# Twenty more pairs of projections by seven half-size products, and weight sums by accumulating transfers

## The chip, the cores and the metric

The kernel runs on one core of one Trainium2 chip. The metric is the device time of one execution in microseconds (us). The kernel before takes 956.11 us, the median of three runs (955.99 to 956.37). The engines are called by the names of the profile: PE multiplies matrices, DVE and ACT work element by element, POOL is GpSimd, SP is the queue that issues most transfers.

## The reference

One decoder block on 512 tokens of 1024 features, with 16 learned meta tokens ahead (528 columns), all in 32-bit floats:

```
xn   = rmsnorm(h, norm1_g)
proj = xn @ w_in      # mq mk mv mi mf mo | gq gk gv ga gr | gate_m gate_g
hm   = mlstm(silu(conv(mq)), silu(conv(mk)), mv, mi, mf);  y_m = headnorm(hm) * sigmoid(mo)
hg   = gla(gq, gk, gv, logsigmoid(ga @ g_a2 + b) / 16);    y_g = headnorm(hg) * silu(gr)
h    = h + (sigmoid(gate_m) * (y_m @ w_branch_m) + sigmoid(gate_g) * (y_g @ w_branch_g)) @ w_out
hn   = rmsnorm(h, norm2_g)
h    = h + (silu(hn @ w_ff_gate) * (hn @ w_ff_up)) @ w_ff_down
out  = rmsnorm(h, final_g)[meta tokens dropped]
```

There are 4 heads in each mixer (key width 128, value width 256), and the channel mixer is 2816 wide.

## The kernel before, in words

**Units.** Every weight matrix is cut into units: one DRAM tile `wst[u]` of 128 x 1024 floats (512 KB) that holds the eight 128 x 128 blocks of one block of 128 output features. Activations lie features on partitions, tokens in columns. Each 32-bit product is made of three matmuls: weights and activations are split into a rounded high part and a rest (`whi`, `wlo`; ACT casts the high part, DVE subtracts), and `mm3` adds high x high, high x rest and rest x high. A unit is 8 such triples of 512 columns (`unit_real`), or 16 of 264 where the meta tokens are needed (`unit_all`).

**Order.** All order is written out by hand: the program emits each engine's instructions in one sequence, and every engine (and each queue) works through its own in that order. SP loads raw weight tiles (`load_raw`, L156) into four rotating buffers, five units ahead; a load waits on SP until the tile four units earlier has been split. `ahead` (L183) puts a split three units ahead of its use. Side work (convolution, gates, heads) is written as generators, and `tick()` after each group of matmuls advances them by a step.

**Stages.** The projections and heads of the first mixer (mLSTM), then those of the second (gated linear attention, GLA) mixed with the merge gates `gm`, `gg` and the branch products `bm`, `bg`, then the output projection, then the channel mixer: 5 blocks of gate and up by plain units, 17 blocks by `pair` (L1077), and the down projection.

**A pair by seven products.** `pair` makes two units that share their input (A is the gate's, B the up's) with seven products of half the depth and half the columns instead of eight: Strassen's scheme in Winograd's form. A product is 4 triples of 256 columns (`seven`, L1048), so a pair is 84 matmuls. The products are called q1, q5, q6, p2, p3, p4, p7. Three PSUM banks hold the sums: bz takes p7 and later p4 on top, bx takes q1, q6, q5 and p3, by takes p2. Because later products are added to the same bank, the state of the bank between them is copied out by ACT (s7: bz after p7; s1: bx after q1; s2: after q6; s5: after q5), and PE may add the next product only when the copy has read the bank. DVE joins the parts (c11, c21, c22), ACT applies Silu, and DVE multiplies gate and up (f). The last product of a pair, p3, is made inside the next pair. The weights of the products are sums of halves of A and B, made by `mix_weights` (L1005) on DVE: two tiles of 128 x 1024 (`st.s`, `st.r`), each half by one addition of 512 columns (L1014, L1015, L1018, L1021), then split like the raw tile of A; of B, only one half (`dh`, `dl`) is split.

Of the kernel before, what the change touches and what calls it, by code (L numbers as in the profile page):

```python
# [15 lines left out]
P = 128  # L16
D = 1024
# [26 lines left out]
TW = 532  # L44
NTT = 60
NSTD = 5
LOGEXP = "natural_log_exp_and_others"
# [3 lines left out]
def unit_order():  # L51

    o = [("gates", 0)]
    m = lambda h: [("mq", h), ("mk", h), ("mv", 2 * h), ("mv", 2 * h + 1), ("mo", 2 * h), ("mo", 2 * h + 1)]
    g = lambda h: [("gq", h), ("gk", h), ("gv", 2 * h), ("gv", 2 * h + 1), ("gr", 2 * h), ("gr", 2 * h + 1)]
    for h in range(H):
        o += m(h)
    for h in range(H):
        o += g(h)
        if h in (1, 2):  # L60
            for i in range(4 * h - 4, 4 * h):
                o += [("gm", i)] if i % 2 == 0 else [("gm", i), ("bm", i - 1), ("bm", i)]
    o += [("gg", i) for i in range(8)] + [("bg", i) for i in range(8)]
    return o


ORDER = unit_order()
NUNITS = len(ORDER) + 8 + 44 + 22
FF0 = len(ORDER) + 8
SW0, SW1 = FF0 + 2 * NSTD, FF0 + 44  # L70

# [13 lines left out]
def hybrid_block(ctx: ExitStack, tc: tile.TileContext, xT, wst, par, con, out):  # L85
# [68 lines left out]
    unit_ix, n_raw = [0], [0]  # L154

    def load_raw(u):  # L156
        while n_raw[0] <= u and n_raw[0] < NUNITS:
            r = raws[n_raw[0]] = wpool.tile([P, D], F32, tag="raw", name=nm("raw"), bufs=4)
            nc.sync.dma_start(r, wst[n_raw[0]])
            n_raw[0] += 1  # L160

    def whi(src):
        t = wpool.tile([P, D], F32R, tag="whi", name=nm("whi"), bufs=5)
        S.copy(t, src)  # L164
        return t

    def wlo(src, hi):
        t = wpool.tile([P, D], F32R, tag="wlo", name=nm("wlo"), bufs=5)
        V.tensor_tensor(t, src, hi.bitcast(F32), ALU.subtract)  # L169
        return t  # L170

    def split_hi(u):
        if u < NUNITS:
            splits[u] = [whi(raws[u])]

    def split_lo(u):
        if u < NUNITS:
            splits[u].append(wlo(raws.pop(u), splits[u][0]))


    plan = {}

    def ahead(u, k):  # L183
        if k == 0:
            load_raw(u + 5)
        if (u, k) in plan:
            for f in plan.pop((u, k)):
                f()
        if not SW0 <= u + 3 < SW1:
            if k == 2:  # L190
                split_hi(u + 3)
            elif k == 4:
                split_lo(u + 3)
# [8 lines left out]
    def unit(outs, ah, al):  # L202

        u = unit_ix[0]
        unit_ix[0] += 1
        w = splits.pop(u)
        for k in range(KT):
            for o, c0, c1 in outs:
                mm3(o, w, k, ah[k], al[k], c0, c1, k == 0, k == KT - 1)
            ahead(u, k)  # L210
            tick()

    def unit_all():
        ps = [bank()[:, :HALF], bank()[:, :HALF]]
        scale = X.scale
        unit([(ps[a], a * HALF, (a + 1) * HALF) for a in range(2)], X.h, X.l)
        return ps, scale

    def unit_real(ah=None, al=None):
        o = bank()  # L220
        if ah is None:
            scale = X.scale
            unit([(o, NM, NT)], X.h, X.l)
            return o, scale
        unit([(o, 0, NS)], ah, al)
        return o

# [24 lines left out]
    cn = apool.tile([P, NCON], F32, name="cn")  # L252
    nc.sync.dma_start(cn, con)
    madd = cn[:, K_MADD:K_MADD + NS]
    m01 = cn[:, K_M01:K_M01 + NS]
# [7 lines left out]
    split_lo(0)  # L263

# [54 lines left out]

    def evac(o, ps):  # L320
# [41 lines left out]
    def gate_rows(ps):  # L362
        sel = gts.sel = apool.tile([P, 8, P], F32R, name="sel")
        G.tensor_copy(sel, cn[:, K_SEL:K_SEL + 8].unsqueeze(2).to_broadcast([P, 8, P]))
# [77 lines left out]
    def conv(box, ps, m, isk):  # L442
# [8 lines left out]
        V.tensor_scalar(a, raw[:, 3 + c0:3 + c0 + n], pr[:, col + 3:col + 4], pr[:, C_CB + m:C_CB + m + 1],  # L451
                        op0=ALU.mult, op1=ALU.add)
# [70 lines left out]
    def head_out(num, d2, gcol, gates, hd, dst):  # L523
# [35 lines left out]
        V.tensor_tensor(t, y0, y0, ALU.mult)  # L559
        V.tensor_tensor(t, t, x, ALU.mult)  # L560
        yield 1
        V.tensor_scalar(t, t, -0.5 / 256.0, 1.5, op0=ALU.mult, op1=ALU.add)
        V.tensor_tensor(y0, y0, t, ALU.mult)
        yield 1
        for vt in range(2):
            y = ts[vt]
            V.tensor_tensor(y, y, y0, ALU.mult)
            yield 1
            hi, lo = tt(F32R, NS), tt(F32R, NS)
            S.copy(hi, y)  # L570
            yield 2
            V.tensor_tensor(lo, y, hi.bitcast(F32), ALU.subtract)
            f = 2 * hd + vt
            dst[0][f], dst[1][f] = hi, lo
# [9 lines left out]
    def mlstm(h, q, k, v, gates, dst):  # L584
        while not gts.ready or q.v is None or k.v is None:
            yield 1
        (qh, ql), (kh, kl) = q.v, k.v
        yield 6
        pb, pm = bank(), bank()
        T.matmul(pb, gts.sel[:, h, :], gts.R, start=True, stop=True)  # L590
        T.matmul(pm, gts.sel[:, H + h, :], gts.R, start=True, stop=True)
# [3 lines left out]
        V.tensor_tensor(dia, pb, madd, ALU.add)  # L595
# [3 lines left out]
        wh = apool.tile([P, WTOT], F32R, tag="wh", name=nm("wh"))  # L599
        wl = apool.tile([P, WTOT], F32R, tag="wl", name=nm("wl"))  # L600
# [46 lines left out]
        for vt in range(2):  # L647
# [8 lines left out]
            if vt == 0:  # L656
# [5 lines left out]
                V.tensor_tensor(em, em, em, ALU.mult)  # L662
# [3 lines left out]
    atts = []  # L666

    def gla_decay(h, gq, gk, dk):
# [12 lines left out]
        b = pr[:, C_A2B + h:C_A2B + h + 1]  # L681
        l, z = tt(), tt()
        for a in range(2):
            c = slice(a * HALF, (a + 1) * HALF)
            act(l[:, c], ps[a], AF.Abs, bias=b)
            V.tensor_scalar(z[:, c], ps[a], b, 0.0, op0=ALU.add, op1=ALU.min)
# [5 lines left out]
        V.tensor_tensor(z, z, l, ALU.subtract)  # L692
# [9 lines left out]
        act(ex[:, 0, :4], bc[:, CH - 1:c4:CH], AF.Exp, scale=1.0 / TAU)  # L702
        act(ex[:, 1, :4], bc[:, mid:c4:CH], AF.Exp, scale=1.0 / TAU)
        act(ex[:, 1, 4:5], bc[:, c4 + 7:c4 + 8], AF.Exp, scale=1.0 / TAU)
# [655 lines left out]
```

## Time and profile before

| | before |
|---|---|
| median of the runs | 956.11 us |
| the profiled execution's own time | 956.21 us |
| its span | 954.2 us |
| PE busy, share of the span | 935.1 us, 98% |
| DVE busy | 601.2 us, 63% |
| ACT busy | 467.6 us, 49% |
| POOL busy | 11.7 us, 1% |
| transferred | 89.40 MB, mean 94 GB/s |

The span runs from the first to the last instruction; the profiled execution's time is 2.0 us longer. Busy time of PE is nearly all of the span, but a matmul's record overlaps the next one's, so the pace of matmuls is read from how many start in a stretch of time. The list of waits names the instruction that an engine stood still for; for SP it is the queue's own waits before it issues a transfer.

### The profile page before, as it was taken

Reading aid. Unit: us, or ns where it says so; the run is one execution under the profiler, and the core shown is the slowest. Engines: PE = TensorE matmul, PEld = TensorE weight load, DVE = VectorE, ACT = ScalarE, POOL = GpSimd, SP = SyncE. Lnnn points to the kernel's source line nnn. Section 1 sums busy time; section 2 is a strip of 40 time slices with the busy share of each in tenths; the row PEclk is TensorE's granted clock in tenths of the full one; section 3 lists DMA queues with packets and bytes.
Section 4 is the critical chain, followed back from the end, with each engine's and each line's share of the span. In section 5 each row is a group of like instructions: output and inputs, shape, how many; then the busy total and the mean of one; then the engine's idle time right before and its main releaser. Section 6 shows DMA issues by size and latency. Waiting matters only on the chain.

```text
span 954.2 us, 13802 instructions
## 1 busy us (share of the span) xinstructions
PE 935.1 (98%) x5687; PEld 832.8 (87%) x5687; DVE 601.2 (63%) x876; ACT 467.6 (49%) x778; POOL 11.7 (1%) x30
## 2 busy tenths in 40 slices
PE   6999999999999999999999999999999999999995
PEld 6988989898988898889888888879999999888885
DVE  6898877674854543452354555798888887842323
ACT  7457667675552544262442234445555555732321
POOL 0000000000000000000000000010000000000000
PEclk9999999999999999999999999999999999999998
DMA  7322221212223232233223343223334233422202
GB/s 262 110 89 69 87 89 45 89 50 84 71 70 94 81 88 85 66 111 89 67 67 110 111 136 129 67 89 105 117 90 129 93 111 112 133 90 87 89 1 88
DMA packets 27294, 89.40 MB, mean 94 GB/s; under 512 B 3040, under 2 KB 5088, under 8 KB 27232
## 3 DMA queue, kind: packets, MB, share of 16 engines
q1 hardware_dynamic: 26144, 87.49, 29.2%
q10 hardware_dynamic: 1088, 1.05, 0.3%
q8 instruction: 44, 0.72, 0.3%
q14 instruction: 18, 0.15, 0.1%
HBM read 86.43 MB, written 2.10 MB: 93 GB/s over the span
## 4 chain that ended last, share of the span: by engine, by line
PE 88%; DVE 8%; ACT 2%; issue 1%; DMA 1%; SPq 0%; DVEq 0%
PE b L198 21%; PE b L200 21%; PE b L199 21%; PE b L1055 6%; PE b L1056 6%; PE b L1054 6%; DVE wlo L169 1%; PE b L767 1%; ACT t L116 1%; PE b L769 1%; PE b L746 1%; PE b L653 1%; PE b L486 1%; PE b L654 1%; DMA t<-xT 1%
## 5 line engine op out<-in xcount | busy, mean ns | idle before, releaser
L198 PE MATMUL b<-t,whi 128*128 128x512 f32 (+2 forms) x1222 | 434.9, 356 | 6.9 <-ACT t L116 6.9
L200 PE MATMUL b<-t,wlo 128*128 128x512 f32 (+2 forms) x1222 | 427.4, 350 | 0.7 <-DVE wlo L169 0.7
L199 PE MATMUL b<-t,whi 128*128 128x512 f32 (+2 forms) x1222 | 427.0, 349 | 0.7 <-DVE t L272 0.7
L198 PEld LDWEIGHTS b<-t,whi 128*128 128x128 f32 x1222 | 231.2, 189 | 36.2 <-ACT t L116 6.8
L200 PEld LDWEIGHTS b<-t,wlo 128*128 128x128 f32 x1222 | 230.8, 189 | 32.6 <-DVE wlo L169 1.1
L199 PEld LDWEIGHTS b<-t,whi 128*128 128x128 f32 x1222 | 231.3, 189 | 30.4 <-DVE t L272 1.0
L169 DVE TENSOR_TENSOR wlo<-raw,whi 128x1024 fp32r<-128x1024 f32 x138 | 168.2, 1223 | 96.0 <-ACT whi L164 95.9
L164 ACT CAST whi<-raw 128x1024 fp32r<-128x1024 f32 x138 | 142.9, 1047 | 17.7 <-issue 7.1
L1056 PE MATMUL b<-t,wlo 128*128 128x256 f32 x408 | 114.6, 281 | 0.0
L1055 PE MATMUL b<-t,whi 128*128 128x256 f32 x408 | 114.5, 281 | 0.0
L1054 PE MATMUL b<-t,whi 128*128 128x256 f32 x408 | 114.2, 280 | 0.0
L1054 PEld LDWEIGHTS b<-t,whi 128*128 128x128 f32 x408 | 76.9, 188 | 0.1
L1055 PEld LDWEIGHTS b<-t,whi 128*128 128x128 f32 x408 | 76.8, 188 | 0.1
L1056 PEld LDWEIGHTS b<-t,wlo 128*128 128x128 f32 x408 | 76.7, 188 | 0.0
L116 ACT ACTIVATE t<-t 128x512 f32<-128x512 f32 (+3 forms) x78 | 43.7, 579 | 45.0 <-DVE t L553 19.5
L116 ACT ACTIVATE t<-b 128x512 f32<-128x512 f32 (+1 forms) x65 | 33.5, 541 | 55.6 <-PE b L200 23.2
L169 DVE TENSOR_TENSOR wlo<-ws,whi 128x1024 fp32r<-128x1024 f32 x34 | 41.5, 1221 | 7.4 <-ACT whi L164 7.4
L116 ACT ACTIVATE t<-f 128x256 f32<-128x256 f32 (+1 forms) x24 | 11.6, 482 | 67.2 <-DVE f L1205 67.2
L1070 ACT COPY t<-b 128x256 f32<-128x256 f32 x51 | 19.0, 373 | 45.6 <-PE b L1056 45.6
L1205 DVE TENSOR_TENSOR f<-f,b 128x512 f32<-128x512 f32 (+1 forms) x9 | 5.7, 629 | 53.9 <-PE b L200 53.9
L164 ACT CAST whi<-ws 128x1024 fp32r<-128x1024 f32 x34 | 35.8, 1052 | 6.3 <-DVE ws L1021 3.5
L791 DVE TENSOR_TENSOR t<-b,t 128x512 f32<-128x512 f32 x16 | 11.1, 691 | 30.8 <-PE b L200 30.8
(200 smaller groups left out, 958.0 us busy)
## 6 DMA issues: line engine op xcount, KB each, us to landing
raw<-wst SPq DMA_DIRECT2D x155, 512.0 KB, 3.5
t<-xT SPq DMA_DIRECT2D x8, 264.0 KB, 5.6
t<-xT SPq DMA_DIRECT2D x8, 256.0 KB, 3.7
out<-t SPq DMA_DIRECT2D x4, 256.0 KB, 2.3
out<-t ACTq DMA_DIRECT2D x4, 256.0 KB, 2.5
cn<-con SPq DMA_DIRECT2D x1, 516.0 KB, 7.3
pr<-par SPq DMA_DIRECT2D x1, 320.0 KB, 7.1
pr<-par SPq DMA_DIRECT2D x1, 44.0 KB, 1.9
```

The costliest lines, as they stand in the source:

```text
L116: S.activation(o, i, func, **kw)
L164: S.copy(t, src)
L169: V.tensor_tensor(t, src, hi.bitcast(F32), ALU.subtract)
L198: T.matmul(o, w_h, ah[:, c0:c1], start=first, stop=False)
L199: T.matmul(o, w_h, al[:, c0:c1], start=False, stop=False)
L200: T.matmul(o, w_l, ah[:, c0:c1], start=False, stop=last)
L486: T.transpose(pb[:, c * P:(c + 1) * P], f[:, c * CH:(c + 1) * CH], ident)
L791: V.tensor_tensor(t, ps, t, ALU.mult)
L1054: T.matmul(o, h, xh_[k], start=start and k == 0, stop=False, skip_group_check=not start)
L1055: T.matmul(o, h, xl_[k], start=False, stop=False, skip_group_check=not start)
L1056: T.matmul(o, l, xh_[k], start=False, stop=k == 3, skip_group_check=not start)
L1070: s7=lambda: S.copy(s[:, lo], bz), s1=lambda: S.copy(s[:, hi], bx), s2=lambda: S.copy(r[:, lo], bx),
```

## The change

The seven-product scheme of the channel mixer is written once for all and used for 20 more pairs: of each GLA head q with k, the two v units and the two r units (12 pairs), and the merge gates `gm` and `gg` two by two (8 pairs). Pairs of q, k and v work on halves of 272 columns (`ALL`), the others on halves of 256 (`REAL`). The order of units in the second mixer changes: all gates `gm` and head 0 come first, then all of `bm`, then heads 1 to 3 interleaved, `gg` and `bg`.

Two of the four half sums of a pair (`ws` first half: B's first half plus A's; `wr` first half: B's two halves) are no longer made by DVE: SP loads one addend from DRAM into the sum's buffer, and POOL issues a transfer that adds the other (`sum_tile`, L198 of the new kernel). `ws` and `wr` have one buffer each, raw tiles three in place of four, `whi` and `wlo` four in place of five. The order of the seven products is now p7, q1, p3 of the pair before, q6, p4, p2, q5 (before: p7, p3 of the pair before, q1, p4, q6, p2, q5).

`begin` loads raw tiles up to `u + 5` and hangs the weight work of the next pair at places of the present one, called by product and step (`("p4", 2)` is p4 after its third triple). Work on `ws` is called b (`b_sum`, `b_hi`, `b_lo`), on the raw tile of A a (`a_hi`, `a_lo`), on half of B d, on `wr` c (`c_hi`, `c_lo`). The work on c is done inside the pair that uses it. New activation sums for the second mixer are made once (`mixed_x`) during the last mLSTM heads. Several small DVE operations go to ACT (first tap of the convolution, clamp of the GLA decay by Relu, squares, state scaling), branch inputs are split later (`parts`), and the two masks share one buffer.

```diff
-    o += [("gg", i) for i in range(8)] + [("bg", i) for i in range(8)]
+    two = lambda n, i: [((n, 2 * i), (n, 2 * i + 1))]
+    g = lambda h: [(("gq", h), ("gk", h))] + two("gv", h) + two("gr", h)
+    bm = lambda i: one(("bm", 2 * i), ("bm", 2 * i + 1))
+    o += two("gm", 0) + two("gm", 1) + g(0) + two("gm", 2) + two("gm", 3)
+    for i in range(4):
+        o += bm(i)
+    q, v, r = ([g(h)[i] for h in range(H)] for i in range(3))
+    o += [q[1], v[1], q[2], r[1], v[2], q[3], r[2], v[3]] + two("gg", 0) + [r[3]]
...
     def load_raw(u):
-            r = raws[n_raw[0]] = wpool.tile([P, D], F32, tag="raw", name=nm("raw"), bufs=4)
+            r = raws[n_raw[0]] = wpool.tile([P, D], F32, tag="raw", name=nm("raw"), bufs=3)
             nc.sync.dma_start(r, wst[n_raw[0]])
...
+    def sum_tile(tag, u, v):
+        t = wpool.tile([P, D], F32, tag=tag, name=nm(tag), bufs=1)
+        (u0, j0), (u1, j1) = u, v
+        nc.sync.dma_start(lr(t, 0), lr(wst[u0], j0))
+        G.dma_start(lr(t, 0), lr(wst[u1], j1), accum_op=ALU.add)
+        return t
...
+    def fetch_mix():
+            st.s = sum_tile("ws", (u + 1, 0), (u, 0))
+    def b_sum(u):
+        st.r = sum_tile("wr", (u + 1, 0), (u + 1, 1))
+        V.tensor_tensor(lr(st.s, 1), lr(st.s, 0), lr(raws[u + 1], 1), ALU.add)
+    def b_hi(u):
+        st.bh = whi(st.s)
+        V.tensor_tensor(lr(st.r, 1), lr(st.s, 1), lr(raws[u], 1), ALU.add)
+    def b_lo(u):
+        l = wlo(st.s, st.bh)
...
+        fetch_mix()
+    def a_lo(u):
+        l = wlo(raws.pop(u), st.ah)
...
+    def c_hi(u):
+        st.ch = whi(st.r)
+    def c_lo(u):
+        l = wlo(st.r, st.ch)
...
+    FIRST = {"s": [(split_hi, ("q6", 1)), (split_lo, ("p4", 0))],
+             "b": [(b_sum, ("p3", 1)), (b_hi, ("q6", 1)), (b_lo, ("p4", 0))]}
+    SECOND = {"s": [(split_hi, ("p4", 2)), (split_lo, ("p2", 2))],
+              "a": [(a_hi, ("p4", 2)), (a_lo, ("p2", 2)), (d_hi, ("p2", 1)), (d_lo, ("q5", 2))],
+              "b": [(b_sum, ("p4", 1)), (b_hi, ("p2", 1)), (b_lo, ("q5", 0))]}
+    def begin(*names):
...
+        load_raw(u + 5)
+        while ready[0] < min(item_ix[0] + 2, len(ITEMS)):
+            kind, v = ITEMS[ready[0]]
+            ready[0] += 1
+            for f, at in tables.pop(0)[kind]:
+                steps.setdefault(at, []).append(lambda f=f, v=v: f(v))
...
+    def pair(names, x, cols, sink):
+        u, steps = begin(*names)
+        w = mixw[u].w
+        bz, bx, by = (bank()[:, :cols[1] - cols[0]] for _ in range(3))
+        e = sink(bz, bx, by)
+        todo = {("p7", 0): ["s5"], ("p7", 2): ["mid", "c22"], ("q6", 0): ["c12"], ("p4", 1): ["fin"]}
+        mine = {("q1", 1): ["s7"], ("p3", 0): ["s1"], ("p4", 0): ["s2"], ("p4", 3): ["c21"], ("q5", 0): ["c11"]}
+        steps.setdefault(("p7", 1), []).append(lambda: c_hi(u))
+        steps.setdefault(("q1", 0), []).append(lambda: c_lo(u))
...
+        seven(bz, w, x, "p7", True, hook, *cols)
+        seven(bx, w, x, "q1", True, hook, *cols)
+        if "p3" in pend:
+            pend.pop("p3")(hook)
...
+        seven(bx, w, x, "q6", False, hook, *cols)
+        seven(bz, w, x, "p4", False, hook, *cols)
+        seven(by, w, x, "p2", True, hook, *cols)
+        seven(bx, w, x, "q5", False, hook, *cols)
...
-        V.tensor_scalar(a, raw[:, 3 + c0:3 + c0 + n], pr[:, col + 3:col + 4], pr[:, C_CB + m:C_CB + m + 1],
-                        op0=ALU.mult, op1=ALU.add)
+        act(a, raw[:, 3 + c0:3 + c0 + n], AF.Identity, scale=pr[:, col + 3:col + 4], bias=pr[:, C_CB + m:C_CB + m + 1])
...
-        elif what == "gv":
-            run(evac_all(head("g", i // 2).vf[i % 2], unit_all()))
-        elif what == "gr":
-            hold(what, i, head("g", i // 2).gates, AF.Silu)
+            if what == "gq":
+                pair(job, X.w, ALL, sink_of((b.q, b.k), False, True))
+            elif what == "gv":
+                pair(job, X.w, ALL, sink_of(b.vf, True, True))
+            elif what == "gr":
+                pair(job, X.w, REAL, sink_of(b.gates, False, False, AF.Silu))
+            else:
...
+                pair(job, X.w, REAL, sink_of({"gm": gm, "gg": gg}[what][i:i + 2], False, False, AF.Sigmoid))
...
-            T.matmul(o, h, xh_[k], start=start and k == 0, stop=False, skip_group_check=not start)
-    def mix_weights(u):
```

`sink_of` does for the new pairs what `evac_pair` did for the channel mixer: s1, s2, s5, s7 and c12 are ACT copies of 256 or 272 columns, c11, c21 and c22 DVE additions, `fin` applies the gate's function.

**SP, two pairs in the middle of the channel mixer.** Before, the queue holds nothing but raw tiles:

```order
L159 DMA raw_1026_5899<-wst 128x1024
L159 DMA raw_1046_6014<-wst 128x1024
L159 DMA raw_1047_6016<-wst 128x1024
L159 DMA raw_1065_6141<-wst 128x1024
L159 DMA raw_1066_6143<-wst 128x1024
```

Now each pair has two raw tiles, then the first addend of `wr` (for the next pair) and of `ws` (for the pair after it):

```order
L176 DMA raw_1242_7036<-wst 128x1024
L176 DMA raw_1243_7038<-wst 128x1024
L202 DMA wr_1253_7086<-wst 128x512
L202 DMA ws_1256_7118<-wst 128x512
L176 DMA raw_1261_7165<-wst 128x1024
L176 DMA raw_1262_7167<-wst 128x1024
L202 DMA wr_1272_7215<-wst 128x512
L202 DMA ws_1275_7247<-wst 128x512
```

The addend of `wr` stands behind the second raw tile. That raw tile (`raw_1262`) takes the buffer of `raw_1242` three tiles earlier, so on SP it waits for the `wlo` of `raw_1242` on DVE.

**ACT, the same pair.** From the pair's start: s5 of the pair before, the cast of `wr`, Silu (mid), s7, s1, Silu (c12), the cast of `ws`, s2, the casts of A and of B's half:

```order
L1303 COPY t_1248_7044<-b_1245_7041 128x256
L181 CAST whi_1270_7183<-wr_1253_7086 128x1024
L132 ACTIVATE t_1250_7046<-t_1250_7046 128x256
L1302 COPY t_1266_7172<-b_1263_7169 128x256
L1302 COPY t_1266_7172<-b_1264_7170 128x256
L132 ACTIVATE t_1250_7046<-b_1245_7041 128x256
L181 CAST whi_1273_7232<-ws_1256_7118 128x1024
L1302 COPY t_1267_7173<-b_1264_7170 128x256
L181 CAST whi_1276_7257<-raw_1242_7036 128x1024
L239 CAST dh_1277_7269<-raw_1243_7038 128x512
```

The cast of `wr`, which before stood at the end of the preparing pair, is now the second instruction of the using pair and stands ahead of s7 and s1.

**DVE, the same pair.** The subtraction for `wr`, the addition into `ws`, the one into `wr`, the subtraction for `ws`, f, c21, the subtraction for A, c11, the one for B's half, and c22:

```order
L186 TENSOR_TENSOR wlo_1271_7196<-wr_1253_7086,whi_1270_7183 128x1024
L218 TENSOR_TENSOR ws_1256_7118<-ws_1256_7118,raw_1243_7038 128x512
L223 TENSOR_TENSOR wr_1272_7215<-ws_1256_7118,raw_1242_7036 128x512
L186 TENSOR_TENSOR wlo_1274_7245<-ws_1256_7118,whi_1273_7232 128x1024
L1298 TENSOR_TENSOR t_1249_7045<-t_1249_7045,t_1250_7046 128x512
L1304 TENSOR_TENSOR t_1268_7174<-b_1263_7169,t_1267_7173 128x256
L186 TENSOR_TENSOR wlo_1278_7274<-raw_1242_7036,whi_1276_7257 128x1024
L1305 TENSOR_TENSOR t_1269_7175<-b_1265_7171,t_1266_7172 128x256
L250 TENSOR_TENSOR dl_1279_7289<-raw_1243_7038,dh_1277_7269 128x512
L1306 TENSOR_TENSOR t_1268_7174<-t_1266_7172,t_1267_7173 128x256
```

Two additions of 512 columns have gone, and the subtraction for A, which frees `raw_1242`, stands behind c21.

More of the change, by code (lines that the diff above doesn't have):

```diff
@@ L172, in split_hi @@
     def split_hi(u):
-        if u < NUNITS:
-            splits[u] = [whi(raws[u])]
+        splits[u] = [whi(raws[u])]
     def split_lo(u):
[L177 to L193, printed above, removed]
+        splits[u].append(wlo(raws.pop(u), splits[u][0]))
@@ L830, in hold, with joined, branch_unit @@
     def hold(what, i, boxes, func):
-        held[what] = held.get(what, []) + [unit_real()]
+        held[what] = held.get(what, []) + [unit_real((what, i))]
         if i % 2:
             run(gates_of(boxes, held.pop(what), func))
-    for what, i in ORDER[1:]:
-        if what == "mq":
+    def joined(y, k):
+        while y[k] is None:
+            tick()
+        if not isinstance(y[k], tuple):
+            parts(y, k)
+    def branch_unit(name, y):
+        for k in range(KT):
+            joined(y, k)
+        return unit_real(name, [a[0] for a in y], [a[1] for a in y])
@@ L954, in hybrid_block @@
     xw = {}
+    hx = [[fpool.tile([P, 2, NS], F32, tag="hx", name=nm("hx"), bufs=2) for _ in range(2)] for _ in range(1)][0]
     def operands():
@@ L976, in operands @@
         for k in (0, 2):
[L977 removed]
+            b1, b2 = hx
             for b, m in ((b1, k), (b2, k + 4)):
```

530 lines of the change are left out of this document (311 added, 219 removed).

## The prediction

> **What bounds the kernel now.** I read the page's busy times first, then the list of waits of PE and of SP, then busy times by stretches of time.
>
> ```profile
> span 954.2 us, 13802 instructions
> PE 935.1 (98%) x5687; PEld 832.8 (87%) x5687; DVE 601.2 (63%) x876; ACT 467.6 (49%) x778; POOL 11.7 (1%) x30
> GB/s 262 110 89 69 87 89 45 89 50 84 71 70 94 81 88 85 66 111 89 67 67 110 111 136 129 67 89 105 117 90 129 93 111 112 133 90 87 89 1 88
> PE b L198 <- ACT t L116: 6.9, 1, 6.9
> PE b L610 <- DVE t L495: 1.1, 1, 1.1
> PE b L1231 <- ACT t L116: 1.0, 1, 1.0
> PE b L199 <- DVE t L272: 0.7, 1, 0.7
> PE b L200 <- DVE wlo L169: 0.7, 1, 0.7
> SPq L159 <- DVE wlo L169: 641.7, 112, 15.2
> SPq L159 <- DVE dl L1029: 122.3, 17, 8.5
> ```
>
> PE stands still for 10.4 us in the whole span, most of it before its first matmul. In between it never waits: the time is the length of PE's stream, and whatever shortens the stream shortens the kernel as long as nothing makes PE wait. The last two rows show something else. SP spends 764 us holding a raw tile's load back until DVE has split the tile that lay in its buffer. Before, that costs nothing, for nothing urgent is queued behind such a load.
>
> The pace of matmuls comes from stretches that hold one shape:
>
> ```profile
> core 0: us, PE busy (x) PEld busy (x) DVE busy (x) ACT busy (x) POOL busy (x), PEclk, DMA share, GB/s
> 300.00:400.00 100.00, 100.00 (x542) 85.80 (x542) 44.44 (x60) 39.48 (x58) 0.00 (x0) 1.00 0.29 85
> 422.50:435.00 12.50, 12.50 (x105) 12.50 (x104) 5.10 (x7) 5.96 (x14) 0.00 (x0) 1.00 0.31 100
> 651.20:818.20 167.00, 167.00 (x1417) 167.00 (x1416) 141.46 (x201) 96.13 (x170) 1.61 (x1) 1.00 0.35 108
> 821.50:926.50 105.00, 105.00 (x454) 85.02 (x454) 42.21 (x54) 37.17 (x62) 0.00 (x0) 1.00 0.24 76
> ```
>
> The second row is units with the meta tokens (264 columns): 12.50 us / 105 = 119 ns a matmul, say 120. The third is the channel mixer's pairs (256): 118 ns. The fourth is the down projection (512): 231 ns. For 272 columns I read 125 ns off the line through 256 and 512.
>
> **What the change removes.** A merge gate or r pair took 48 matmuls of 512, 11.09 us; as 84 of 256 it takes 9.91 us. Twelve such pairs save 14.1 us. A v pair took 96 of 264, 11.52 us, against 84 x 125 ns = 10.50 us: four save 4.1 us. A q and k pair took 24 of 512 and 48 of 264, 11.30 us: four save 3.2 us. Together PE's stream gets 21.4 us shorter. Without new waits that is 956.2 - 21.4 = 934.8 us.
>
> **What it adds: one chain per pair.** Follow `wr` through a channel mixer pair, by the program's order. DVE ends a_lo, which frees the oldest raw buffer. Only then does SP issue the second raw load, and behind it the first addend of `wr`. When this has landed, POOL issues the accumulating transfer. When that has landed, ACT's c_hi can start, and it is the second instruction of the next pair on ACT. Behind it are queued mid, s7 and s1, and PE may not add q6 to bx before s1 has read it. On DVE, c_lo waits for c_hi, and behind c_lo stand b_sum, then (after ACT's b_hi) b_lo, fin, c21, and the next a_lo, which starts the chain again. So it is a loop, and a pair can't be shorter than its length. The durations:
>
> ```profile
> 565.40 0.33 SPq L159 DMA_DIRECT2D raw<-wst  x1
> 565.78 0.42 SPq L915 DMA_DIRECT2D t<-xT  x1
> raw<-wst SPq DMA_DIRECT2D x155, 512.0 KB, 3.5
> t<-xT SPq DMA_DIRECT2D x8, 256.0 KB, 3.7
> out<-t SPq DMA_DIRECT2D x4, 256.0 KB, 2.3
> cn<-con SPq DMA_DIRECT2D x1, 516.0 KB, 7.3
> pr<-par SPq DMA_DIRECT2D x1, 44.0 KB, 1.9
> L164 ACT CAST whi<-ws 128x1024 fp32r<-128x1024 f32 x34 | 35.8, 1052 | 6.3 <-DVE ws L1021 3.5 <-DVE ws L1018 1.7 <-ACT t L1070 0.3
> L169 DVE TENSOR_TENSOR wlo<-ws,whi 128x1024 fp32r<-128x1024 f32 x34 | 41.5, 1221 | 7.4 <-ACT whi L164 7.4
> L1018 DVE TENSOR_TENSOR ws<-ws,raw 128x512 f32<-128x512 f32 x17 | 11.6, 685 | 0.0
> L1066 DVE TENSOR_TENSOR t<-t,t 128x512 f32<-128x512 f32 x17 | 11.6, 685 | 1.3 <-ACT t L116 1.3
> L1072 DVE TENSOR_TENSOR t<-b,t 128x256 f32<-128x256 f32 x17 | 7.2, 424 | 1.1
> L1070 ACT COPY t<-b 128x256 f32<-128x256 f32 x51 | 19.0, 373 | 45.6 <-PE b L1056 45.6
> L116 ACT ACTIVATE t<-t 128x256 f32<-128x256 f32 x19 | 8.0, 422 | 0.1
> ```
>
> From a_lo's end to the addend's issue: 0.38 us, the step between a raw tile's issue and that of the 256 KB transfer behind it (first two rows). That same 256 KB transfer, behind a 512 KB one, lands 3.7 us after its issue; alone one lands in 2.3 us. The accumulating transfer has no row: POOL issues none before. It brings 256 KB and must read the 256 KB it adds to, so the nearest row is that of 512 KB, 3.5 us, which I take. Its bounds are 1.9 us (44 KB, the shortest landing here) and 7.3 us (516 KB in the crowd of the start). Then come the rows of the same operations before: c_hi 1.05 (L164), c_lo 1.22 (L169), b_sum 0.69 (L1018), b_hi 1.05, b_lo 1.22, fin 0.69 (L1066), c21 0.42 (L1072), a_lo 1.22: 7.56 us. b_add runs on DVE beside b_hi, and the sum of `ws`, issued right behind `wr`, lands while c_hi and c_lo run. The loop is 0.38 + 3.7 + 3.5 + 7.56 = 15.1 us. PE's side of it is shorter: c_hi 1.05, mid 0.42 (L116), s7 and s1 0.75 (L1070), then 24 matmuls of q6 and p4, 2.83, reach c21 after 5.0 us, where DVE arrives after 5.9.
>
> The Trainium skill, in "DMA: Bandwidth & Descriptors", section "Anatomy of one DMA — SWDGE (gpsimd) path", gives a transfer from POOL about 2.0 us plus its bytes at 436 GB/s: 2.6 us here, an estimate that leaves out the addition. By it the loop would be 0.9 us shorter and the sum below 31 us lower; no row here shows such a transfer.
>
> A channel mixer pair needs 84 x 118 ns = 9.91 us of PE, so each loses 5.2 us. There are 17, of which 16 follow a pair: **83 us**. A pair of the second mixer needs 10.15 us on average (12 of 9.91, 8 of 10.50). Its loop lacks fin on DVE (-0.7) but has the heads' work in it. In the stretch from 300 to 400 us, DVE is busy 44.4 us, of which about 18 splits of 1.22 are 22; the other 22 us per 100 are 2.3 us per pair, and half of a period is DVE's half of the loop: +1.2. That makes 15.6 us, and 18 of the 20 pairs lose 5.45 each: **98 us**.
>
> **The clock.** The pause of PE, about 5 us in one piece before q6, has a price of its own:
>
> ```profile
> 8.54 0.42 PE L200 MATMUL b<-t,wlo 128*128 128x264 f32 x1
> 8.76 0.42 PE L198 MATMUL b<-t,whi 128*128 128x264 f32 x1
> 944.82 0.70 PE L1231 MATMUL b<-t,ones 128*128 128x256 f32 x2 [0.96 <-ACT t L116]
> 945.60:948.50 2.90, 0.00 (x0) 0.00 (x0) 1.86 (x5) 0.84 (x2) 0.00 (x0) 1.00 0.00 1
> 948.70:954.00 5.30, 0.00 (x0) 0.00 (x0) 2.01 (x4) 0.00 (x0) 0.00 (x0) 0.51 0.57 198
> ```
>
> After the last matmul (at 945.5 us) the granted clock is full until 948.5 and 0.51 from 948.7 on, and at the kernel's start, after idling, matmuls start 0.22 us apart in place of 0.12. At half clock q6 and p4 take 5.2 us, PE reaches c21 after 7.4 us and the loop grows by 1.5 us. One drop doesn't tell that every pause of 5 us brings one; I take six in ten, 34 x 1.5 x 0.6 = **31 us**. The Trainium skill ("TensorE: Matmul & The Clock Gate", section "Part 1: The HAM clock gate (the "warmup" mystery)") has the clock halved after an idle window of about 3.4 us that runs freely, which would hit some pauses of 5 us and spare others.
>
> **What costs nothing.** The new pairs' DVE and ACT work (a third cast and subtraction, sums, copies) lies beside PE or in the loop. `mixed_x` is made in a stage where, as in the row from 300 to 400 us, DVE is busy less than half; without that cover its roughly 20 us would be added. The operations moved from DVE to ACT end no wait of PE's list. Two additions of 0.69 and about 0.8 us less per channel mixer pair help a DVE on which PE did not wait.
>
> **The sum.** 956.2 - 21.4 + 83 + 98 + 31 = 1147 us; against the median, 0.1 us lower, the same.
>
> **Rivals.** *The sums land in time: faster, 935 us.* From p4's end to the next q6 PE has p2, q5, p7, q1 and p3, 60 matmuls or 7.1 us. Fixed in the chain are c21, a_lo, the issue, c_hi, mid, s7 and s1: 4.2 us. If both landings together take under 2.9 us, nothing stops. For it: the amount to move is small and the transfer engines were 0.35 busy. Against it: no landing here is under 1.9 us, and there are two in a row. 7 in 100.
>
> *Short landings: 1016 us.* With 2.3 us (the row alone, not behind a raw tile) and 1.9 us the loop is 12.1 us: 16 x 2.2 and 18 x 2.5 are 81 us, and pauses of 2.2 us leave the clock alone, as the 2.9 us at the end did. 956.2 - 21.4 + 81. For it: two small transfers. Against: the first is behind 512 KB. 17 in 100 for the region from 960 to 1060.
>
> *POOL's transfer starved: 1296 us.* At 7.3 us the loop grows by 3.8 us, 34 times 129 us, and the clock falls in every pause (+20). For it: POOL has issued no transfer here, so that its issue may be slow or held up. Against: one core, 2 MB per 15 us (about 140 GB/s), where the first slice of the span moved 262. 9 in 100 for all above 1230.
>
> *The clock stays up: 1116 us*, or falls each time, 1167 us. Both lie in the forecast's own range.
>
> **Numbers.** Forecast 1147 us, its own range 1060 to 1230, 65 in 100. Slower by more than 0.2% (what a measurement of this kernel can tell): 0.91, all cases but the first rival (0.07) and 0.02 for a time within 0.2%. The range that should hold the time 8 times in 10 goes down to the short landings and up past the forecast's own, 1015 to 1260 us.
>
> **What would show it.** Right: PE waits for s1 (an ACT copy of 256 or 272 columns out of a bank) some 35 times for 3 to 6 us; ACT's idle time is ended by POOL's transfer into `wr`; SP's raw loads still wait for DVE's subtraction, and the addend of `wr` is issued within a microsecond after; a channel mixer pair takes about 15 us in place of 9.9; the granted clock falls below 1 in the pair stages. Wrong: if PE's pairs run at 9.9 us, the chain is broken at a place I misread, most likely the SP queue; if PE waits for `wlo` or c21 instead, DVE is the bound, not the transfers; if landings are right and the pauses are short, the loop's members overlap more than I took them to.

## The result, and the profile after

The changed kernel takes 1271.32 us (median of four runs, 1270.85 to 1277.14) against 956.19 us for the kernel before: a ratio of 1.331, 95% interval 1.327 to 1.334. The profiled execution is the longest of the four, 1277.14 us, 0.5% above the median. The forecast was 1147 us, its range 1015 to 1260 us. The direction and the place were right, the size was not: 191 us more were forecast, 315 came.

The page of the changed kernel, its busy times, two of its groups and its transfers (the last number of a transfer's row is the median from issue to landing):

```profile
span 1275.4 us, 15442 instructions
PE 1005.8 (79%) x6119; PEld 923.2 (72%) x6119; DVE 653.6 (51%) x970; ACT 545.1 (43%) x951; POOL 77.4 (6%) x107
L181 ACT CAST whi<-wr 128x1024 fp32r<-128x1024 f32 x37 | 38.6, 1044 | 285.4 <-DMA wr<-wst 285.4
L203 POOL DMA_DIRECT2D wr<-wst x37 | 32.1, 867 | 750.9 <-DMA wr<-wst 586.5
raw<-wst SPq DMA_DIRECT2D x155, 512.0 KB, 3.7
ws<-wst SPq DMA_DIRECT2D x37, 256.0 KB, 4.7
ws<-wst POOLq DMA_DIRECT2D x37, 256.0 KB, 5.1
wr<-wst SPq DMA_DIRECT2D x37, 256.0 KB, 3.9
wr<-wst POOLq DMA_DIRECT2D x37, 256.0 KB, 4.0
```

PE, which had been busy 98% of the span, is busy 79%, and no other engine took its place: DVE is down to 51%, ACT to 43%. Everybody waits for somebody. Who waits for whom stands in the list of waits of the same execution (total us, times, longest us):

```profile
PE b L342 <- ACT t L401: 122.3, 20, 9.3
PE b L342 <- ACT t L1302: 94.6, 17, 7.7
PE b L851 <- POOL sel L848: 10.5, 1, 10.5
DVE t L407 <- PE b L344: 30.3, 17, 3.9
DVE t L1304 <- PE b L344: 18.3, 16, 1.7
SPq L176 <- DVE wlo L186: 687.3, 86, 22.7
SPq L176 <- DVE t L1305: 228.9, 15, 17.7
```

L401 and L1302 are here s1, the copy out of bx after q1. PE waits for it once in each of the 37 pairs, 5.9 us on average. ACT makes it late because c_hi is queued ahead of it, and c_hi waits for the transfer into `wr` 37 times (285.4 us, the row of L181 above). SP's raw loads wait for splits by DVE. The last row names c11 (L1305), but in the loop below the load starts while c11, next after a_lo on DVE, is still running, so it was a_lo that let it go. One loop, in the timeline of a channel mixer pair (start, us, engine and line):

```profile
1066.17 1.21 DVE L186 TENSOR_TENSOR wlo<-raw,whi 128x1024 fp32r<-128x1024 f32 x1
1067.41 0.33 SPq L176 DMA_DIRECT2D raw<-wst  x1
1067.84 0.38 SPq L202 DMA_DIRECT2D wr<-wst  x1
1072.40 0.89 POOL L203 DMA_DIRECT2D wr<-wst  x1 [14.93 <-DMA wr<-wst]
1076.50 1.04 ACT L181 CAST whi<-wr 128x1024 fp32r<-128x1024 f32 x1 [7.52 <-DMA wr<-wst]
1077.58 1.22 DVE L186 TENSOR_TENSOR wlo<-wr,whi 128x1024 fp32r<-128x1024 f32 x1 [8.14 <-ACT whi L181]
1078.45 0.58 PE L342 MATMUL b<-t,whi 128*128 128x256 f32 x1 [5.60 <-ACT t L1302]
1080.56 1.22 DVE L186 TENSOR_TENSOR wlo<-ws,whi 128x1024 fp32r<-128x1024 f32 x1 [0.43 <-ACT whi L181]
1083.35 1.22 DVE L186 TENSOR_TENSOR wlo<-raw,whi 128x1024 fp32r<-128x1024 f32 x1
```

This is the forecast's chain member by member: a_lo ends at 1067.38, SP issues the raw load 0.03 us later and the addend of `wr` behind it, POOL issues when that has landed, c_hi starts when POOL's has landed, PE comes back after 5.6 us, and the next a_lo closes the loop 17.2 us after the last.

Averaged over all loops of a kind (differences of such rows), with the forecast's members beside them:

| from, to (us) | forecast | channel mixer, 16 loops | second mixer, last 12 | second mixer, first 6 |
|---|---|---|---|---|
| a_lo's end to POOL's issue | 4.1 | 5.25 | 5.22 | 5.39 |
| POOL's issue to c_hi's start | 3.5 | 4.01 | 4.12 | 4.11 |
| c_hi's start to c_lo's end | 2.3 | 2.30 | 2.68 | 2.51 |
| c_lo's end to b_sum's end | 0.7 | 0.73 | 1.08 | 1.39 |
| b_sum's end to b_hi's start | 0 | 0.08 | 0.96 | 0.82 |
| b_hi's start to b_lo's end | 2.3 | 2.30 | 2.92 | 2.47 |
| b_lo's end to a_lo's end | 2.3 | 3.16 | 3.72 | 5.06 |
| loop | 15.1 | 17.8 | 20.7 | 21.7 |

Of the 5.25 us of the first row, in the channel mixer, 0.45 pass before SP issues the addend, 4.17 until it has landed, and 0.63 between the landing and POOL's issue. The last had no term in the forecast.

Where the 321 us of span went can be read off the starts of all matmuls. Take from each step its shape's pitch (231, 124.5, 119 and 118 ns for 512, 272, 264 and 256 columns; for the heads' few other shapes, 231 ns in proportion to the columns). A rest above 0.35 us is a stall; the smaller rests add up to what PE lost by a slow pace. What is left of the span is the stream at its pitch, with some 16 us ahead of the first matmul and behind the last.

| us | before | after | all sums by DVE (below) |
|---|---|---|---|
| stalls | 4.5 | 262.6 | 51.8 |
| slow pace | 39.4 | 123.5 | 52.1 |
| rest: the stream at its pitch | 910.3 | 889.3 | 889.3 |
| span | 954.2 | 1275.4 | 993.2 |

PE's stream did get 21.0 us shorter. Stalls took 258 us more, the slow pace 84.

### The profile page after: what moved, and what is told of

Read it like the earlier page. It is cut to its first block, busy times and chain, and to the rows that moved or that the text cites. A ratio compares the mean times of both kernels' runs of the same rounds, so it can differ in the third digit from the quotient of the medians.

```text
span 1275.4 us, 15442 instructions
## 1 busy us (share of the span) xinstructions
PE 1005.8 (79%) x6119; PEld 923.2 (72%) x6119; DVE 653.6 (51%) x970; ACT 545.1 (43%) x951; POOL 77.4 (6%) x107
## 4 chain that ended last, share of the span: by engine, by line
PE 37%; DMA 23%; ACT 14%; DVE 13%; issue 11%; SPq 1%; POOLq 0%; POOL 0%; DVEq 0%; ACTq 0%
DMA wr<-wst 22%; PE b L302 8%; PE b L300 8%; PE b L301 8%; PE b L342 5%; ACT t L132 4%; DVE wlo L186 4%; ACT whi L181 4%; PE b L343 4%; PE b L344 4%; ACT L132 1%; DMA ws<-wst 1%; ACT t L1302 1%; ACT L130 1%; DVE t L699 1%
## 5 line engine op out<-in xcount | busy, mean ns | idle before, releaser
L342 PE MATMUL b<-t,whi 128*128 128x256 f32 (+1 forms) x888 | 281.9, 317 | 226.0 <-ACT t L401 122.3
L342 PEld LDWEIGHTS b<-t,whi 128*128 128x128 f32 x888 | 188.3, 212 | 235.2 <-ACT t L401 126.8
L301 PE MATMUL b<-t,whi 128*128 128x512 f32 (+2 forms) x806 | 286.5, 355 | 0.8 <-DVE t L468 0.7
L300 PE MATMUL b<-t,whi 128*128 128x512 f32 (+2 forms) x758 | 270.5, 357 | 8.5 <-ACT t L132 6.5
L302 PE MATMUL b<-t,wlo 128*128 128x512 f32 (+2 forms) x758 | 267.4, 353 | 7.3 <-DVE wlo L186 7.3
L344 PE MATMUL b<-t,wlo 128*128 128x256 f32 (+1 forms) x888 | 271.7, 306 | 0.0
L343 PE MATMUL b<-t,whi 128*128 128x256 f32 (+1 forms) x888 | 271.3, 305 | 0.0
L343 PEld LDWEIGHTS b<-t,whi 128*128 128x128 f32 x888 | 189.8, 214 | 0.3
L186 DVE TENSOR_TENSOR wlo<-wr,whi 128x1024 fp32r<-128x1024 f32 x37 | 45.3, 1224 | 251.9 <-ACT whi L181 251.9
L301 PEld LDWEIGHTS b<-t,whi 128*128 128x128 f32 x806 | 154.6, 192 | 22.3 <-DVE t L468 1.4
L300 PEld LDWEIGHTS b<-t,whi 128*128 128x128 f32 x758 | 145.9, 193 | 28.7 <-ACT t L132 6.5
L181 ACT CAST whi<-wr 128x1024 fp32r<-128x1024 f32 x37 | 38.6, 1044 | 285.4 <-DMA wr<-wst 285.4
L181 ACT CAST whi<-raw 128x1024 fp32r<-128x1024 f32 x118 | 122.8, 1044 | 20.6 <-issue 11.1
L132 ACT ACTIVATE t<-t 128x512 f32<-128x512 f32 (+4 forms) x118 | 66.6, 588 | 36.2 <-DVE t L641 6.8
L203 POOL DMA_DIRECT2D wr<-wst x37 | 32.1, 867 | 750.9 <-DMA wr<-wst 586.5
L342 PE MATMUL b<-t,dh 128*128 128x256 f32 (+1 forms) x148 | 55.2, 373 | 0.0
L181 ACT CAST whi<-ws 128x1024 fp32r<-128x1024 f32 x37 | 38.8, 1048 | 37.2 <-DVE ws L218 26.2
L343 PE MATMUL b<-t,dh 128*128 128x256 f32 (+1 forms) x148 | 52.8, 357 | 0.0
```

Of the source, the lines that this page charges most:

```text
L132: S.activation(o, i, func, **kw)
L203: G.dma_start(lr(t, 0), lr(wst[u1], j1), accum_op=ALU.add)
L300: T.matmul(o, w_h, ah[:, c0:c1], start=first, stop=False)
L301: T.matmul(o, w_h, al[:, c0:c1], start=False, stop=False)
L302: T.matmul(o, w_l, ah[:, c0:c1], start=False, stop=last)
L342: T.matmul(o, h, xh_[k][:, c0:c1], start=start and k == 0, stop=False, skip_group_check=not start)
```

## The experiments

**All sums by DVE.** The transfers into `ws` and `wr` are taken out, the twenty pairs stay.

```diff
-        nc.sync.dma_start(lr(t, 0), lr(wst[u0], j0))
-        G.dma_start(lr(t, 0), lr(wst[u1], j1), accum_op=ALU.add)
+        V.tensor_tensor(lr(t, 0), lr(raws[u0], j0), lr(raws[u1], j1), ALU.add)
```

> The changed kernel with all four half sums of a pair made by DVE again, out of the raw tiles; no transfer into ws or wr. The twenty new pairs, three raw buffers and the new order of products stay. Theory (the loop through wr's two transfers is the whole loss): the PE waits for s1 and for sel go, PE's stream is 934.8 us; DVE gets 37 x 2 x 0.69 = 51 us more. In a mixer pair DVE then has about 8.4 us of pair work and 2.2 us of heads' work against 10.15 us of PE, so up to 0.5 us x 20 may come back: 935 to 955 us, 945 the likeliest. Rival (the new pairs themselves, their copies and the order of products, are the loss): over 1100 us, with PE still waiting for s1.

Measured: 995.58 us, ratio 1.041 (1.039 to 1.042). Page and waits:

```profile
PE 930.8 (94%) x6119; PEld 851.5 (86%) x6119; DVE 693.1 (70%) x1044; ACT 544.2 (55%) x951; POOL 12.9 (1%) x33
```

```profile
PE b L341 <- ACT t L402: 9.9, 2, 8.7
PE b L341 <- ACT t L400: 7.3, 5, 4.3
PE b L301 <- DVE wlo L186: 7.3, 4, 3.6
PE b L730 <- DVE wl L892: 5.6, 1, 5.6
PE b L851 <- DVE t L778: 4.5, 1, 4.5
PE b L341 <- ACT t L1301: 3.4, 4, 1.1
```

276 of the 315 us are the two accumulated sums. The waits for s1 (L400, L1301) fall from 217 to 11 us, and a channel mixer pair takes 10.3 us (from the first to the last split of `wr`, by 16). The new pairs, three raw buffers and the new order cost 39 us by themselves, which I had not expected: by the table above, 47 us of stalls and 13 of slow pace more than before, against 21 us of shorter stream.

**The second raw load behind `wr`.** Sums by transfers as in the change; only SP's order differs.

```diff
-        load_raw(u + 5)
+        load_raw(u + 5 if len(names) == 1 else u + 4)
+        if len(names) == 2:
+            steps.setdefault(("p2", 0), []).append(lambda: load_raw(u + 5))
```

> The changed kernel with one thing moved: in a pair the second raw load is issued after p4, behind the first addend of wr, in place of ahead of it. The sums stay with the transfers. Theory (the raw load that waits for a_lo holds wr's addend back): a_lo leaves the loop; what is left is c_lo to addend to accumulating transfer to c_hi to c_lo: 0.1 + 2.3..4.6 + 4.1 + 1.05 + 1.22 = 8.8 to 11.1 us against 9.9 to 10.5 us of PE. 934.8 + 0..1.2 x 34 + 10 for the wait for sel: 945 to 985 us, 960 the likeliest; POOL's transfers still take about 4 us each. Rival (POOL's transfers or the slow clock are the cause by themselves): above 1150 us.

Measured: 1064.5 us, ratio 1.112 (1.111 to 1.114). One load moved brings 207 us, so the raw load that waits for a_lo does hold the loop together; but 105 us more than expected remain. DVE's waits, and the timeline of one pair:

```profile
DVE ws L218 <- DMA ws<-wst: 129.1, 29, 6.1
DVE wlo L186 <- ACT whi L181: 66.6, 70, 5.9
```

```profile
834.28 1.23 DVE L186 TENSOR_TENSOR wlo<-ws,whi 128x1024 fp32r<-128x1024 f32 x1 [0.43 <-ACT whi L181]
835.53 0.33 SPq L202 DMA_DIRECT2D ws<-wst  x1
839.72 0.86 POOL L203 DMA_DIRECT2D ws<-wst  x1 [5.21 <-DMA ws<-wst]
846.00 0.69 DVE L218 TENSOR_TENSOR ws<-ws,raw 128x512 f32<-128x512 f32 x1 [6.01 <-DMA ws<-wst]
847.85 1.23 DVE L186 TENSOR_TENSOR wlo<-ws,whi 128x1024 fp32r<-128x1024 f32 x1 [0.43 <-ACT whi L181]
```

The sum of `ws` has a loop of its own: its one buffer is free when b_lo has read it (835.51), the addend takes 4.2 us to POOL's issue, POOL's transfer 6.3, then sum, b_hi and b_lo: 13.6 us. A channel mixer pair takes 12.9 us on average. The loop of `wr` had hidden it.

**The same, with `ws` summed by DVE.** Only `wr` still comes by transfers.

```diff
-            st.s = sum_tile("ws", (u + 1, 0), (u, 0))
...
+        st.s = wpool.tile([P, D], F32, tag="ws", name=nm("ws"), bufs=1)
+        V.tensor_tensor(lr(st.s, 0), lr(raws[u + 1], 0), lr(raws[u], 0), ALU.add)
```

> The kernel with the late second raw load, and besides it DVE makes the sum of ws (out of the raw tiles); only wr's first half still comes by two transfers. Theory (once a_lo is out of wr's loop, the loop of ws is the bound: b_lo, addend 4.1, accumulating transfer 6.2, sum, b_hi, b_lo): the wait of b_sum for ws, 129 us in all, goes; what is left is c_lo, addend, accumulating transfer, c_hi, c_lo, 10.1 to 11.6 us: 995 to 1030 us, 1010 the likeliest, a channel mixer pair at 10.3 to 11.2 us. Rival (the transfers into wr bound it just as well): 1055 to 1070 us.

Measured: 1005.57 us, ratio 1.051 (1.050 to 1.053), a channel mixer pair at 10.2 us. As expected: two loops, one behind the other. One accumulated sum a pair still gains nothing over DVE's own (995.58).

**No accumulating transfers.**

```diff
-        G.dma_start(lr(t, 0), lr(wst[u1], j1), accum_op=ALU.add)
```

> The changed kernel without POOL's accumulating transfers: the first halves of ws and wr hold one addend alone, so the weight sums of all 37 pairs are left incomplete; the rest is done as before. Theory: the transfer's landing of 4.1 us leaves the loop of each of the about 35 pairs that wait (-144 us), the pauses of PE come down from 5.6 to 1.5 us, too short for the clock to fall (-0.7 to -1.5 us each), and the wait for sel goes (-10): 1070 to 1120 us, 1090 the likeliest. If the hold on SP and the first addend alone made the loss, it would stay at about 1270 us; if POOL's transfers were all of it, 935 us.

Measured: 1068.82 us, ratio 1.118 (1.116 to 1.120), just below the range; ACT's waits:

```profile
ACT whi L181 <- DMA wr<-wst: 127.9, 37, 8.0
```

From a_lo's end to c_hi's start the channel mixer's loops take 4.64 us in place of 9.26, from b_lo's end to a_lo's 2.29 in place of 3.16, since the clock mostly stays up after the shorter pauses (granted clock of the whole span 0.962, in the changed kernel 0.881). The loop falls from 17.8 to 12.4 us: POOL's transfer is 4.6 us of the chain, its hand-over with it, and the hold by the raw load is in what remains.

**POOL's transfers without the addition.** They overwrite the first addend.

```diff
-        G.dma_start(lr(t, 0), lr(wst[u1], j1), accum_op=ALU.add)
+        G.dma_start(lr(t, 0), lr(wst[u1], j1))
```

> The changed kernel with POOL's transfers into ws and wr written without the addition: they overwrite the first addend, so all weight sums of the pairs are left incomplete. It parts the price of the adding from that of a second transfer issued by POOL (4.0 us from POOL's issue to c_hi). If the adding costs (the target has to be read too, as my choice of the 512 KB row supposed): the second transfer lands in about 3 us and 34 loops lose 1 us each, 1225 to 1250 us, 1240 the likeliest. If a transfer from POOL takes 4 us whatever it does: 1265 to 1280 us.

Measured: 1241.08 us, ratio 1.298 (1.295 to 1.300), as expected for a price of the adding. Transfers of the page:

```profile
ws<-wst POOLq DMA_DIRECT2D x37, 256.0 KB, 3.3
wr<-wst POOLq DMA_DIRECT2D x37, 256.0 KB, 3.1
```

256 KB written by POOL land in 3.1 us into `wr`, added in 4.0; into `ws` in 3.3 and 5.1.

**c_hi and c_lo behind s1.**

```diff
-        steps.setdefault(("p7", 1), []).append(lambda: c_hi(u))
-        steps.setdefault(("q1", 0), []).append(lambda: c_lo(u))
+        steps.setdefault(("p3", 0), []).append(lambda: c_hi(u))
+        steps.setdefault(("p3", 1), []).insert(0, lambda: c_lo(u))
```

> The changed kernel with c_hi and c_lo moved behind s1 (from p7 and q1 to p3), nothing else. Rival (the order on ACT, c_hi ahead of s7 and s1, is what costs): PE no longer waits for s1 and the kernel comes to 960 to 1000 us. Theory (the loop is on SP, the transfers and DVE, and c_hi ahead of s1 only decides where PE stands still): PE's waits move from s1 to the weights of q5 (wlo) or to s2, the pair's period stays the loop's 17 us less at most the 1 us that DVE waited for PE at c21: 1220 to 1275 us, 1245 the likeliest.

Measured: 1202.86 us, ratio 1.257 (1.255 to 1.259); PE's waits:

```profile
PE b L342 <- ACT t L1302: 72.7, 17, 6.5
PE b L342 <- ACT t L402: 63.8, 19, 8.1
```

L402 is s2, and L1302 holds s1 and s2 alike: PE now stands ahead of the next product into bx, q5. The loop stays, 16.9 us in the channel mixer (0.95 less), but 18.3 in the second mixer's last 12 (2.4 less), which is why it came out below the range. So c_hi at the head of ACT's queue is not the cause of the loop. From b_lo's end to a_lo's, where DVE no longer waits for PE at c21, it gains 1.1 us in both (3.16 to 2.03, 3.72 to 2.59). The second mixer gains 1.3 us more between c_hi's start and b_hi's (4.71 to 3.37; 3.11 and 3.14 in the channel mixer), where the heads' work stands in the same queues. c_lo moved together with c_hi, so the run doesn't part ACT's order from DVE's.

**The pauses filled with matmuls.** 36 matmuls into `by`, which p2 overwrites.

```diff
+        if warm:
+            h, d = w["q1"][0], x["q1"][0]
+            for i in range(36):
+                T.matmul(by, h[:, :P], d[0][:, cols[0]:cols[1]], start=i == 0, stop=i == 35)
         seven(bx, w, x, "q6", False, hook, *cols)
```

> The changed kernel with 36 matmuls more (256 or 272 columns, 4.3 to 4.5 us, into by's bank, which p2 overwrites) ahead of q6 in every pair that follows a pair, 34 times: they fill most of PE's pause of 5 to 7 us, so that it is short. Nothing else changes and the result is the same. Theory (the half clock after a pause lengthens the loop, since c21 waits for p4): the waits of DVE for PE at c21, 18 us in the channel mixer's pairs and 30 us in the others, go nearly all: 1215 to 1240 us, 1225 the likeliest. Rival (the half clock is covered by the rest of the loop): 1265 to 1275 us. If the added matmuls come into the way of PE where a pause is shorter than they are: above 1275 us.

Measured: 1257.59 us (1251.51 to 1261.37), ratio 1.314 (1.311 to 1.318): 14 us less, not 46. Granted clock in the channel mixer's pairs, the changed kernel first, then this one (the clock is the third number from the right):

```profile
846.00:1132.00 286.00, 192.89 (x1345) 189.59 (x1346) 117.81 (x160) 89.18 (x163) 28.77 (x32) 0.80 0.44 116
```

```profile
846.00:1120.00 274.00, 238.83 (x1897) 234.72 (x1896) 118.91 (x165) 91.59 (x170) 25.29 (x29) 0.97 0.47 119
```

The clock is back, and from b_lo's end to a_lo's the loops get shorter: 3.16 to 2.31 us, 3.72 to 2.97, 5.06 to 4.15. That is about 0.8 us a pair, 28 us in 34. Of it 0.25 us a loop returns between a_lo's end and POOL's issue (5.25 to 5.50). The whole loops are 0.5 to 0.9 us shorter (17.3, 20.0 and 20.9 us), 22 us in 34, and the two profiled executions lie 26 us apart. But that of the changed kernel is the longest of its four and this one the shortest of its own, so what the half clock costs is known only to between 14 and 26 us.

**The copy for `sel` by DVE**, since PE waited 10.5 us for a copy that POOL made behind two transfers.

```diff
-        G.tensor_copy(sel, cn[:, NS + h:NS + 8:H].unsqueeze(2).to_broadcast([P, 2, P]))
+        V.tensor_copy(sel, cn[:, NS + h:NS + 8:H].unsqueeze(2).to_broadcast([P, 2, P]))
```

> The changed kernel with the copy that makes sel done by DVE instead of POOL, so that it isn't queued behind POOL's transfers. PE's wait of 10.5 us for sel goes; with the sums by DVE PE waited 4.5 us for DVE at the same matmul, so I expect that wait back. If the time goes with it: 1262 to 1267 us. Rival (the first loops of wr go on while PE stands at sel, and PE waits for s1 that much longer): 1268 to 1274 us.

Measured: 1268.74 us, ratio 1.326 (1.323 to 1.329), which overlaps the change's own 1.327 to 1.334. PE waited 4.3 us at that matmul in place of 10.5. The wait was real, its 10 us were not for the taking; whether the first loops swallow it stays open.

**What remains without the transfers.** Three steps on the kernel with all sums by DVE: `mixed_x` begun one head earlier; then besides it either the pair's last product made ahead of a branch unit, or c_hi and c_lo behind s1; and, on this last one, the last r pair one place earlier.

```diff
-            if i == 3:
+            if i == 2:
                 run(mixed_x())
```

> The kernel with all sums by DVE, and the activation sums of the second mixer (mixed_x) begun one head of the first mixer earlier. Theory (of what remains above 935 us, the stalls of PE between 176 and 219 us, 18.6 us and some 8 us of half clock behind them, come from mixed_x's DVE and ACT work that stands between the last mLSTM head's): 965 to 980 us, 972 the likeliest. Rival (the stalls are the last head's own, moved against PE by the shorter and reordered stream): 990 to 1000 us.

```diff
     def branch_unit(name, y):
+        left("s5", "mid", "c22", "p3", "c12", "fin")
```

> As the kernel before it in this list, and the last product of a pair that is followed by a branch unit is made before the unit waits for the heads' parts, not inside the unit. Theory (the wait of 8.7 us for s5 at 521 us is s5 queued on ACT behind casts that wait for the last head): 3 to 9 us less than without, 965 the likeliest. Rival (the unit would have waited for the last head by itself): within 2 us of it.

The step on c is the diff shown above for c_hi and c_lo.

> All sums by DVE, mixed_x begun one head earlier, and c_hi and c_lo behind s1. Of the 988 us of the kernel without the last step some 9 us are waits of PE for s1 of 0.5 to 3.1 us each, and some of the half clock behind them. Theory (ACT's order makes these): 975 to 983 us, 980 the likeliest. Rival (they are ACT's load from the heads): 986 to 990 us.

```diff
-    o += [q[1], v[1], q[2], r[1], v[2], q[3], r[2], v[3]] + two("gg", 0) + [r[3]]
+    o += [q[1], v[1], q[2], r[1], v[2], q[3], r[2], v[3], r[3]] + two("gg", 0)
```

> As the kernel before it in this list, and the last head's r pair stands one pair earlier, ahead of the first gg pair. Theory (the 8.7 us that PE waits for the last product at about 513 us are the last head being late for the first branch unit): the head ends up to 10 us earlier and the wait goes, 9 to 11 us less, about 970 us. Rival (the head's work goes by PE's groups of matmuls and by earlier waits, not by the place of its r pair): within 3 us of the other.

Measured: 988.08 us (ratio 1.033, 1.031 to 1.035), 989.3 (1.033 to 1.036), 1006.43 (1.051 to 1.054) and 1004.87 (1.050 to 1.053). The first shows that `mixed_x` cost 7.5 us, a third of the 24 that I put on it. Busy times from 160 to 200 us, the kernel before first, then the one with all sums by DVE (after the length: PE, PEld, DVE, ACT, POOL, each with its count):

```profile
160.00:200.00 40.00, 40.00 (x249) 35.97 (x248) 28.14 (x48) 27.68 (x56) 1.05 (x2) 1.00 0.20 66
```

```profile
160.00:200.00 40.00, 32.47 (x203) 29.24 (x202) 33.33 (x67) 21.98 (x50) 0.00 (x0) 0.91 0.11 40
```

DVE was busy 70% there before, not "less than half". The flush and the r pair changed nothing (the rivals). With the flush PE waits 7.3 us for the head's parts (L823) in place of 8.7 us for s5, and with the r pair earlier the 8.7 us stay: it is the last head that is late, wherever the product stands. And c_hi behind s1, a gain where transfers are late, costs 18 us where they are not, against both of my ranges: PE now waits 17 times for a copy out of a bank in the channel mixer's pairs (L1301, 6.9 us in all) and nine times for a split (5.0 us). Such a pair goes from 10.3 to 10.6 us, which is 5 of the 18 us; the others lie in the second mixer and were not taken apart. No kernel tried here comes below 956 us.

## Why the prediction was wrong, step by step

**PE's stream, -21.4 us: right**, 21.0 by the matmuls counted after the fact; the pitches are those of the forecast.

**The loop: right as a mechanism.** Its release by a_lo, its two landings in a row and its hold on s1 are in the timeline, and the loop is broken when the load moves or the transfers go. It was sized too small, and that is the step that failed. With the clock's share the forecast had 16.0 us for a channel mixer loop and 16.5 for one of the second mixer; 17.8 came, and 20.7 (the last 12) and 21.7 (the first 6). 16 x 1.8 + 12 x 4.2 + 6 x 5.2 = 111 us, in two terms:

- *The landings, 3.7 + 3.5, the larger miss: 60 of the 111 us.* From a_lo's end to c_hi the loop takes 9.3 us (9.5 in the first six), where I added 0.38 + 3.7 + 3.5 = 7.6, and all 34 loops have this stretch: 16 x 1.7 + 12 x 1.8 + 6 x 1.9. The addend is 1.2 us later at POOL, 0.6 of it between its landing and POOL's issue. The accumulating transfer is 0.5 us slower than the 512 KB row I took for it; the run without addition puts 0.9 us of its 4.0 on adding. The Trainium skill ("DMA: Bandwidth & Descriptors", section "Anatomy of one DMA — SWDGE (gpsimd) path") would have made it 2.6 us, an estimate from about 2.0 us plus the bytes at 436 GB/s, without the addition. The plain transfer took 3.1, the adding one 4.0, so the row was the better guide.
- *The heads' work in the second mixer's loop, +1.2: 49 us.* I counted DVE's work alone, and only for DVE's half. ACT's work (gates, activations, casts of the heads) stands in the same queue as b_hi, c_hi and a_hi. The run with c late shows that the place of c_hi and c_lo among that work makes 1.3 us a pair of it; how the rest divides between ACT, DVE and the slow pace of PE was not taken apart.

The channel mixer's pairs have next to nothing beside the landings (2 us). The 111 us, read from an execution 6 us longer than the median, are most of the 124 by which the forecast fell short. The rest was not taken apart; PE's list has waits that I had at nothing, 10.5 us for `sel`, 9.2 for s5 (L403) and 7.3 for splits.

**The clock, 31 us: too much, and near only by two errors.** I had it fall in six of ten pauses and cost 1.5 us each time. It fell after each of the 38 stalls above 4.05 us, and the run that filled the pauses takes 0.8 us from the step that it hits and 14 to 26 us from the time, 0.4 to 0.8 a pause. That it is so little because DVE comes to c21 late anyway is argued, not shown.

**What costs nothing: wrong.** Without any transfer the change is still 39 us slower than before and 61 above the shorter stream. I took DVE's share from the stretch 300 to 400 us for a stage that ran at 70%. The lost look-ahead (a split two items ahead of its use and three raw buffers, before three ahead and four) I passed over; that it causes the remaining waits for splits is argued, not shown.

**The rivals.** Short landings (2.3 and 1.9 us) and sums in time: no, 4.2 and 3.9 us in the channel mixer's loops. The row of 2.3 us was of `out<-t`, a transfer out to DRAM; the loads of 256 KB before (`t<-xT`) took 3.7. POOL's transfer starved at 7.3 us: no, 4.0, though its number, 1296 us, lies nearest to the result. That `ws` lands beside c_hi and c_lo was true, but only as long as `wr` was slower.

## What to carry to other kernels

A tile with one buffer that is filled by two transfers in a row is a loop: from the last reader, through the queue, both landings and the work, back to the reader. Add it up before trusting that a sum made by transfers is free, and see what stands ahead of its first transfer in the queue, for a kind of load that had been held back harmlessly, 764 us in all, became the pacemaker. When two engines' in-order queues are members of the loop, count everything else that both of them have to do in between, and take shares of time from the stretch in question. Two buffers for the sums, or four raw buffers, which might open these loops, were not run.

## What the hardware showed

**Pauses and the clock.** In the changed kernel and the twelve of the experiments, take all stalls that began at full pace and had no other stall within seven matmuls. The pace of the matmuls behind them is full or about half (1.8 to 1.9 times the pitch). Of 51 stalls of 1.5 to 2.1 us one was followed by the half pace, of 52 between 2.1 and 3.3 us 20, of 14 between 3.3 and 4.05 us 7, and of 139 longer ones all. In the changed kernel the half pace then lasted 3.1 to 7.1 us after all but one of the 38 stalls above 4.05 us, neighbours or not. The Trainium skill ("TensorE: Matmul & The Clock Gate", section "Part 1: The HAM clock gate (the "warmup" mystery)") has an idle window of about 3.4 us that runs freely. With 3.4 us, shorter pauses would have left the clock alone, and 21 of those up to 3.3 us did not. A free-running window of some 2 us, an estimate from these counts, would give what is seen here: some of the pauses from 2 us on and all from about 4. I had read from the end of the kernel before that pauses of 2.2 us leave the clock alone; of those between 2.1 and 3.3 us, three in five did.

**Transfers issued by POOL.** 256 KB land in 3.1 to 3.3 us, with addition in 4.0 to 5.1, and in 6.2 for `ws` in the kernel with the late raw load, where two raw tiles and an addend are issued within some 2 us of it; that these are the reason was not tested. Each issue holds POOL for 0.87 us (L203), and POOL waits with its whole queue for the first addend.
